# Split-precision decoder trunk: token halves of the last output column in PSUM tiles of their own, another division of the norms' work between VectorE and ScalarE, and an earlier start of the FFN's second k-group

## The chip, the cores and the metric

The kernel runs on one core of one Trainium2 chip. The metric is the device time of one execution in microseconds (us); shown are the median of three runs and, beside it, one profiled execution. Engines are named as in the profile: PE (TensorE's matmuls), DVE (VectorE), ACT (ScalarE), POOL (GpSimd) and SP (SyncE, which issues the DMAs).

## The reference

Two layers of a decoder trunk on 256 tokens of width 2048 in float32, every sub-layer behind an RMS norm that a conditioning vector shifts, scales and gates:

```
def rms_norm(x, g, eps=1e-6):
    return x * lax.rsqrt(jnp.mean(x * x, axis=-1, keepdims=True) + eps) * g

for layer in range(DEPTH):                                   # DEPTH = 2
    mod = (silu(c) @ ada_w[layer] + ada_b[layer])[:, None, :]
    sh_m, sc_m, g_m, sh_f, sc_f, g_f = jnp.split(mod, 6, axis=-1)
    hm = rms_norm(x, norm_mix_g[layer]) * (1.0 + sc_m) + sh_m
    y = ab_mixer(hm, ...) if layer == 0 else cd_mixer(hm, ...)    # w_in -> heads -> w_out
    x = x + (1.0 + g_m) * y
    hf = rms_norm(x, norm_ffn_g[layer]) * (1.0 + sc_f) + sh_f
    x = x + (1.0 + g_f) * swiglu(hf, w_gate, w_up, w_down)        # D_FF = 5632
```

## The kernel before

**Linears.** Every float32 product is made of three matmuls on rounded halves: `hi*h + hi*l + lo*h`. A weight slab (two k-tiles of 128 rows, 512 columns, 512 KB) is loaded into a `raw` tile by SP's queue, copied to `hi` by ACT (L311) and subtracted to `lo` by DVE (L316); of `raw` there are four buffers, of `hi` and `lo` three each. In `dense_as` the tokens stand still in PE and the weights stream: a PSUM tile `accps` of two banks holds the two token halves of 128, and a slab costs 12 matmuls of 512 columns (2 k-tiles, 3 products, 2 halves). A linear goes over its output in column blocks of 512. In the last block (`b == 3`) of a linear that adds to the residual stream, called the tail here, the last two slabs are done together, 12 matmuls for token half 0 first and then 12 for half 1.

**Residual and norm.** `residual` multiplies the PSUM tile by a gate (L848), adds to `xr` (L852) and has ACT take the squares for the next norm (`Stats`, L876, with Sqrt at L885 and DVE's reciprocal at L890). `Norm` then makes the next linear's stationary tiles, per k-tile: `scale` multiplies tokens by the reciprocal root (the first 512 columns on DVE, L916, the others on ACT, L914), PE transposes 128x128 pieces into a `pm` tile (PSUM, one bank, L149), ACT's `high` makes `h` (L920) and DVE's `low` makes a value `t` (L926) and `l = t - h` (L927). Both of these read the same PSUM tile:

```
h = A.activation(self.hs[k][0][:, dst], ps, AF.Identity, bias=..., scale=self.gs[k])
V.tensor_scalar(t, ps, self.gs[k], modcol(self.layer, self.sh, k), op0=OP.mult, op1=OP.add)
V.tensor_tensor(l[:, dst], t, h[:, dst].bitcast(F32), op=OP.subtract)
```

`head(cc)` does this for the first four k-tiles of token half `cc`, inside the first two slabs of the next linear; `pair(j)` does it for k-tiles 2j and 2j+1 of both halves, one pair per slab from then on. This happens in three places, which the text calls by their reciprocal roots: f0 (`rstdf`, after the output projection of layer 0, before FFN 0), m1 (`rstdm`, after FFN 0, before layer 1's mixer) and f1 (`rstdf`, after layer 1's output projection, before FFN 1).

**FFN 0 in two k-groups.** FFN 0 reads its weights for the first eight k-tiles over twelve column blocks (group 1), then for the other eight (group 2), adding to the sums kept in SBUF. `grouped(..., early=1)` queues the `pair`s of group 2 at the start of the last block of group 1.

**Order.** Python order within priorities gives each engine's program. `tc.issue_after(x)` keeps an instruction behind `x` on its engine. `pace` and `npace` are a list and a count by which a slab's split is kept behind the norm work of the pair before it, so that the splits don't run ahead of the pairs. `W_AHEAD` is the priority lead of a slab's load and split.

## Time and profile before

| what | value |
|---|---|
| median of three runs | 2621.95 us (2621.33 to 2623.5) |
| the profiled execution's own time | 2620.44 us |
| its span, first to last instruction | 2618.7 us |
| mean granted clock of PE, as a share of full speed | 0.992 |
| PE, DVE, ACT busy | 2564.7, 1887.3, 1244.0 us |
| DMA | 672.97 MB, 257 GB/s on the mean |

The span is from the first to the last instruction on the core; the execution's own time is 1.7 us more. The waits of an engine are idle time by what ended it. A window's row gives an engine's busy time with its count of instructions and the granted clock. In a timeline row, instructions of one line that follow each other are joined (x4), and the bracket gives the idle time before the first and what ended it.

### The profile page before, as it was taken

How to read it: one execution, taken by the hardware profiler on the slowest of the kernel's cores; microseconds unless marked ns; L12 is line 12 of the kernel's file. 1: busy time of each engine (PE TensorE's matmuls, PEld its weight loads, DVE VectorE, ACT ScalarE, POOL GpSimd, SP SyncE). 2: the span in 40 equal slices, each digit the busy share in tenths (PEclk: the TensorE clock that was granted, in tenths of full speed). 3: DMA queues.
4: the chain of work that ended last, by engine and by line, in shares of the span. 5: the costliest groups of instructions: out<-in, count | busy, mean ns of one | idle time of the engine just before them, and what ended most of it. 6: DMA issues, size and time to landing. Idle time of an engine off the chain costs nothing.

```text
span 2618.7 us, 35776 instructions
## 1 busy us (share of the span) xinstructions
PE 2564.7 (98%) x13669; PEld 2198.0 (84%) x13669; DVE 1887.3 (72%) x2046; ACT 1244.0 (48%) x1566; POOL 5.2 (0%) x19
## 2 busy tenths in 40 slices
PE   6999999999999999999999999999999999999999
PEld 5999899988787888888888799998688888888887
DVE  6899887889777887777777687767674455544554
ACT  4534866645544444344444545544544443344443
POOL 0000000000000000000000000000000000000000
PEclk8999999999999999999999999999999999999999
DMA  8998677889697989999898588788676666666665
GB/s 313 336 337 292 187 216 225 271 276 329 224 329 271 325 299 312 319 316 310 299 303 313 176 270 279 249 266 277 196 256 193 187 191 199 201 190 191 190 202 162
DMA packets 307798, 672.97 MB, mean 257 GB/s; under 512 B 24016, under 2 KB 26538, under 8 KB 307626
## 3 DMA queue, kind: packets, MB, share of 16 engines
q1 hardware_dynamic: 307338, 670.60, 78.1%
q8 instruction: 107, 1.75, 0.3%
q14 instruction: 65, 0.53, 0.1%
q10 hardware_dynamic: 288, 0.08, 0.0%
HBM read 668.46 MB, written 2.13 MB: 256 GB/s over the span
## 4 chain that ended last, share of the span: by engine, by line
PE 94%; DVE 2%; ACT 2%; DMA 2%; issue 1%; SPq 0%; DVEq 0%; ACTq 0%
PE accps L158 71%; PE accps L358 18%; PE pm L158 4%; PE pm L149 1%; DMA blk<-in_ada_w 1%; ACT h L920 1%; DVE lo L316 1%; ACT hi L311 1%; DVE t L926 0%; DMA raw<-in_ab_w_in 0%; DMA xr<-in_x 0%; DMA hb<-in_ssd_a_log 0%; DVE blk L316 0%; DVE l L927 0%; PE pm L687 0%
## 5 line engine op out<-in xcount | busy, mean ns | idle before, releaser
L311 ACT ACTIVATE hi<-raw 128x1024 fp32r<-128x1024 f32 (+1 forms) x875 | 913.8, 1046 | 1188.6 <-PE accps L158 922.1
L316 DVE TENSOR_TENSOR lo<-raw,hi 128x1024 fp32r<-128x1024 f32 (+1 forms) x875 | 1052.8, 1206 | 565.2 <-ACT hi L311 556.8
L158 PE MATMUL accps<-hi,h 128*128 128x512 f32 x1908 | 524.2, 394 | 13.6 <-ACT hi L311 6.4
L158 PE MATMUL accps<-hi,l 128*128 128x512 f32 x1908 | 518.1, 392 | 0.0
L158 PE MATMUL accps<-lo,h 128*128 128x512 f32 x1908 | 515.0, 391 | 0.0
L206 DVE SCALAR_TENSOR_TENSOR acc<-araw,ct,acc 128x1024 f32<-128x1024 f32 (+2 forms) x377 | 465.5, 1235 | 14.5 <-DMA araw<-in_ada_w 13.6
L158 PEld LDWEIGHTS accps<-hi,h 128*128 128x128 f32 x1908 | 354.1, 188 | 93.6 <-ACT h L920 15.1
L158 PEld LDWEIGHTS accps<-hi,l 128*128 128x128 f32 x1908 | 357.6, 188 | 76.6 <-DVE l L927 2.8
L158 PEld LDWEIGHTS accps<-lo,h 128*128 128x128 f32 x1908 | 358.5, 189 | 75.0 <-issue 0.2
L158 PE MATMUL accps<-hi,blk 128*128 128x512 f32 x1664 | 413.6, 390 | 0.0
L358 PE MATMUL accps<-h,lo 128*128 128x256 f32 x1408 | 380.3, 285 | 3.1 <-DVE lo L316 3.1
L358 PE MATMUL accps<-h,hi 128*128 128x256 f32 x1408 | 380.0, 285 | 2.2 <-ACT h L473 1.7
L358 PE MATMUL accps<-l,hi 128*128 128x256 f32 x1408 | 378.7, 285 | 0.0
L158 PEld LDWEIGHTS accps<-hi,blk 128*128 128x128 f32 x1664 | 311.7, 188 | 64.4
L358 PEld LDWEIGHTS accps<-h,hi 128*128 128x128 f32 x1408 | 262.4, 192 | 4.8 <-ACT h L473 1.8
L358 PEld LDWEIGHTS accps<-h,lo 128*128 128x128 f32 x1408 | 261.8, 192 | 4.7 <-DVE lo L316 3.8
L358 PEld LDWEIGHTS accps<-l,hi 128*128 128x128 f32 x1408 | 261.8, 192 | 1.1 <-issue 0.2
L158 PE MATMUL accps<-lo,blk 128*128 128x512 f32 x832 | 223.5, 389 | 0.0
L158 PEld LDWEIGHTS accps<-lo,blk 128*128 128x128 f32 x832 | 156.1, 188 | 32.4
L512 DVE TENSOR_TENSOR blk<-accps,blk 128x1024 f32<-128x1024 f32 x40 | 48.7, 1218 | 5.4 <-PE accps L158 5.2
L848 DVE TENSOR_TENSOR blk<-accps,gate 128x1024 f32<-128x1024 f32 (+1 forms) x27 | 29.7, 1104 | 29.6 <-PE accps L158 28.1
L926 DVE TENSOR_SCALAR t<-pm,gs,mod 128x256 f32<-128x256 f32 (+1 forms) x60 | 29.3, 488 | 25.5 <-ACT h L920 25.5
(247 smaller groups left out, 1098.1 us busy)
## 6 DMA issues: line engine op xcount, KB each, us to landing
araw<-in_ada_w SPq DMA_DIRECT2D x323, 512.0 KB, 5.5
raw<-in_ffn_w_gate SPq DMA_DIRECT2D x176, 512.0 KB, 4.4
raw<-in_ffn_w_up SPq DMA_DIRECT2D x176, 512.0 KB, 4.5
raw<-in_ffn_w_down SPq DMA_DIRECT2D x176, 512.0 KB, 4.8
raw<-in_ab_w_in SPq DMA_DIRECT2D x130, 512.0 KB, 5.1
raw<-in_cd_w_in SPq DMA_DIRECT2D x96, 512.0 KB, 4.8
raw<-in_ab_w_out SPq DMA_DIRECT2D x64, 512.0 KB, 5.6
raw<-in_cd_w_out SPq DMA_DIRECT2D x32, 512.0 KB, 5.7
```

Source lines behind the costliest of these rows:

```text
L149: T.transpose(dst, src, ident)
L158: return T.matmul(o, a, b, start=first, stop=last, skip_group_check=True)
L206: V.scalar_tensor_tensor(acc, r, ct[nr][:, g:g + 1], acc, op0=OP.mult, op1=OP.add)
L311: A.activation(hi, raw, AF.Copy)
L316: wlast[1] = V.tensor_tensor(lo, raw, hi.bitcast(F32), op=OP.subtract)
L358: dense_mm[0] = T.matmul(acc[:, n, :], a[:, n * P:(n + 1) * P], b, start=first and n % 2 == 0, stop=final, skip_group_check=True)
L512: V.tensor_tensor(dst, acc, dst, op=OP.add)
L848: V.tensor_tensor(y[:, c, :], acc[:, c, :], g[:, None, :].to_broadcast([P, c.stop - c.start, 512]), op=OP.mult)
L920: return A.activation(self.hs[k][0][:, dst], ps, AF.Identity, bias=modcol(self.layer, self.sh, k), scale=self.gs[k]).ins
L926: V.tensor_scalar(t, ps, self.gs[k], modcol(self.layer, self.sh, k), op0=OP.mult, op1=OP.add)
```

## The change

1. In the tail each token half has a `pm` tile of its own in place of one `accps` tile, and half 0's multiply and add no longer share a tile with half 1. At the end of the kernel, half 0 is added and stored, then half 1.
2. `prefetch` loads and splits three slabs of the next linear before the tail's first add (in `before`, two slabs, one of them split by DVE behind that add, and the third later). The second and the third have buffers of their own (`own`) and are not paced.
3. `head` has two `pm` tiles with two transposes each; the first 512 columns of token half 1 are scaled by ACT.
4. In `pair`, DVE alone reads the transposes: two values, then ACT copies them to `h`, then two `low`s. The scale of the next 512 columns goes with each pair, so a pair's transposes are there one slab earlier.
5. `grouped` has `early=2`: the pairs of group 2 are queued two blocks (eight slabs) ahead, without pace.

```diff
-            after = pace[2 * npace[0] - 1] if 0 < 2 * npace[0] <= len(pace) else None
+            after = pace[2 * npace[0] - 1] if 0 < 2 * npace[0] <= len(pace) and not own else None
...
+    def prefetch(w, c0):
+        for j in range(3):
+            ready.append(wslab(w, 2 * j, 2, c0, 512, W_AHEAD, own=j > 0))
+        return wlast[1].ins
...
-        acc = psA.tile([P, 1024], F32, tag="acc", name="accps").rearrange("p (n t) -> p n t", n=2)
+        if tail:
+            accs = [pm(), pm()]
...
-                made.append((run, *wslab(w, run[0][0], len(run), c0, 512, ahead, own=begin and j == 1)))
+                made.append((run, *(ready.popleft() if ready else wslab(w, run[0][0], len(run), c0, 512, ahead))))
...
-                if begin and j == 0:
-                    head(n)
+                if begin and (n, j) in ((0, 0), (0, len(ops) - 2)):
+                    head(int(j > 0))
...
+        if isinstance(acc, list):
+            with (tc.issue_after(after) if after else ExitStack()):
+                add(0)
+            if store:
+                nc.sync.dma_start(out[0, 0:P, c0:c0 + 512], xr[:, 0, c0:c0 + 512])
+                add(1)
+                nc.sync.dma_start(out[0, P:S, c0:c0 + 512], xr[:, 1, c0:c0 + 512])
+            else:
+                stats.add(0, b)
+                stats.end(0)
+                stats.second = lambda: add(1)
+            return
...
+        def value(self, k, ps, t):
+            return V.tensor_scalar(t, ps, self.gs[k], modcol(self.layer, self.sh, k), op0=OP.mult, op1=OP.add).ins
...
-                ps = pm()
+                two = [pm(), pm()]
...
+                ts = [t1(), t1()]
                 for i in range(2):
-                    k = 2 * j + i
-                    pace.append((self.high(k, ps[:, i * S:(i + 1) * S], slice(0, S)),
-                                 self.low(k, ps[:, i * S:(i + 1) * S], slice(0, S))))
-                self.last = pace[-1]
+                    self.value(2 * j + i, ps[:, i * S:(i + 1) * S], ts[i])
+                for i in range(2):
+                    act = A.activation(self.hs[2 * j + i][0], ts[i], AF.Copy).ins
+                for i in range(2):
+                    dve = self.low(2 * j + i, ts[i], slice(0, S))
+                self.scale(c + 1, j % 2)
...
+        after = prefetch(ffn_w_gate[0], 0) if b == 3 else None
...
-    hf = grouped(fblocks, FGROUPS, 0, 3, makef, finishf, F_RATES, (LAGS[-1], LAGS[-1]), normf.head, 1)
+    hf = grouped(fblocks, FGROUPS, 0, 3, makef, finishf, F_RATES, (LAGS[-1], LAGS[-1]), normf.head, 2)
```

DVE's program around m1's first add, before: `lo` rows are splits of slabs (of the tail, at first), `blk<-raw,blk` the split of a prefetched slab with its own buffers, L848 and L852 the multiply and the add of a token half.

```order
L316 TENSOR_TENSOR lo<-raw,hi 128x1024 [waits DMAHW4_49,PE_49,Activation_49]
L316 TENSOR_TENSOR lo<-raw,hi 128x1024 [waits DMAHW6_49,PE_49,Activation_49]
L848 TENSOR_TENSOR blk<-accps,gate 128x512 [waits PE_49]
L852 TENSOR_TENSOR xr<-blk,xr 128x512 [waits DVE_49]
L316 TENSOR_TENSOR blk<-raw,blk 128x1024 [waits DMAHW7_49,Activation_49]
L890 RECIPROCAL rstdm_12342<-rstdm_12342 128x1 [waits Activation_49]
L916 TENSOR_SCALAR t_13268<-xr,rstdm_12342 128x256 [waits DVE_49]
```

The same place after the change, where L869 and L872 are the multiply and the add and L951 the scale; the four splits are those of the first slab with its own buffers, of the tail's last slab, of the second slab with its own buffers, and of the prefetched slab in the common buffers:

```order
L316 TENSOR_TENSOR blk<-raw,blk 128x1024 [waits DMAHW7_49,Activation_49]
L316 TENSOR_TENSOR lo<-raw,hi 128x1024 [waits DMAHW4_49,PE_49,Activation_49]
L316 TENSOR_TENSOR blk<-raw,blk 128x1024 [waits DMAHW0_49,Activation_49]
L316 TENSOR_TENSOR lo<-raw,hi 128x1024 [waits DMAHW6_49,PE_49,Activation_49]
L869 TENSOR_TENSOR blk<-pm,gate 128x512 [waits PE_49]
L872 TENSOR_TENSOR xr<-blk,xr 128x512 [waits DVE_49]
L924 RECIPROCAL rstdm_12345<-rstdm_12345 128x1 [waits Activation_49]
L951 TENSOR_SCALAR t_13280<-xr,rstdm_12345 128x256 [waits DVE_49]
```

So three splits of prefetched slabs stand ahead of the first add, where one stood and another followed it; the text calls the two with their own buffers p1 and p2 and the one in the common buffers p0, and the tail's last slab sn.

PE's program in m1 at a pair's place, before: L149 are the transposes into a `pm` tile, L158 the matmuls of a slab.

```order
L158 MATMUL accps<-lo,h_13225 128x512 x2
L149 MATMUL pm<-ident,t_13394 128x128 [waits Activation_49]
L149 MATMUL pm<-ident,t_13394 128x128
L149 MATMUL pm<-ident,t_13396 128x128 [waits Activation_49]
L149 MATMUL pm<-ident,t_13394 128x128
L149 MATMUL pm<-ident,t_13396 128x128 x2
L149 MATMUL pm<-ident,t_13394 128x128
L149 MATMUL pm<-ident,t_13396 128x128
L158 MATMUL accps<-hi,h_13227 128x512 [waits Activation_49]
```

And after:

```order
L158 MATMUL accps<-lo,h_13247 128x512 x2
L149 MATMUL pm<-ident,t_13369 128x128
L149 MATMUL pm<-ident,t_13390 128x128
L149 MATMUL pm<-ident,t_13369 128x128
L149 MATMUL pm<-ident,t_13390 128x128
L158 MATMUL accps<-hi,h_13249 128x512 [waits Activation_49]
```

Before, the eight transposes of two pairs stand right ahead of the matmuls that need the first of them. After, four transposes stand between two slabs' matmuls, and they belong to the pair of the slab after the next.

PE's program in FFN 0 where the first matmul of group 2 comes, before (`h_8407` is the first tile of group 2, and `t_8494` and `t_8496` are sources of its transposes):

```order
L149 MATMUL pm<-ident,t_8494 128x128 [waits Activation_49]
L149 MATMUL pm<-ident,t_8496 128x128 [waits Activation_49]
L149 MATMUL pm<-ident,t_8494 128x128
L149 MATMUL pm<-ident,t_8496 128x128
L158 MATMUL accps<-lo,h_7401 128x512 [waits DVE_49]
...
L158 MATMUL accps<-hi,h_7405 128x512 [waits Activation_49]
...
L158 MATMUL accps<-lo,h_7407 128x512 x2
L158 MATMUL accps<-hi,h_8407 128x512 [waits PE_49,Activation_49]
```

And after, where `h_8325` is that tile:

```order
L158 MATMUL accps<-hi,h_7412 128x512 [waits Activation_49]
L158 MATMUL accps<-hi,h_7412 128x512
L158 MATMUL accps<-hi,h_7414 128x512 x2
L158 MATMUL accps<-hi,l_7413 128x512 x2
L158 MATMUL accps<-hi,l_7415 128x512 x2
L158 MATMUL accps<-hi,h_8325 128x512 [waits Activation_49]
```

The transposes of group 2 have left the last block of group 1; they stand in the block ahead of it, four after each of its slabs.

## Rows read from the trace of the kernel before

**Rows 1.** The page: the span, and busy time of each engine.

```profile
span 2618.7 us, 35776 instructions
PE 2564.7 (98%) x13669; PEld 2198.0 (84%) x13669; DVE 1887.3 (72%) x2046; ACT 1244.0 (48%) x1566; POOL 5.2 (0%) x19
```

**Rows 2.** PE's waits: line, releaser, us in total, times, longest us.

```profile
PE pm L149 <- DVE t L916: 9.6, 3, 3.2
...
PE accps L158 <- ACT hi L311: 6.4, 5, 2.5
PE accps L158 <- ACT h L920: 6.4, 14, 0.6
```

**Rows 3.** Windows: length; PE, PEld, DVE, ACT, POOL busy (instructions); PEclk, DMA share, GB/s.

```profile
696.87:716.00 19.13, 14.52 (x60) 10.37 (x60) 16.41 (x38) 11.42 (x24) 0.00 (x0) 0.91 0.23 64
...
828.04:851.69 23.65, 18.25 (x77) 13.95 (x76) 17.87 (x25) 14.20 (x19) 0.00 (x0) 0.93 0.50 158
...
1452.42:1491.43 39.01, 32.77 (x134) 23.14 (x135) 30.53 (x59) 23.56 (x41) 0.00 (x0) 0.91 0.34 102
...
1866.02:1901.70 35.68, 29.42 (x119) 20.46 (x119) 27.51 (x56) 20.90 (x39) 0.00 (x0) 0.90 0.32 89
```

**Rows 4.** The chain that ended last, and PE's timeline at eight transposes.

```profile
1170.23 43.55 PE accps L158 x192
...
1474.23 1.04 PE L149 MATMUL pm<-ident,t 128*128 128x128 f32 x8
```

**Rows 5.** Timeline of m1's head: start and length in us.

```profile
1451.80 0.61 PE L158 MATMUL accps<-lo,blk 128*128 128x512 f32 x2
1452.45 0.69 DVE L848 TENSOR_TENSOR blk<-accps,gate 128x512 f32<-128x512 f32 x1 [4.03 <-PE accps L158]
...
1455.18 0.62 DVE L916 TENSOR_SCALAR t<-xr,rstdm 128x256 f32<-128x256 f32 x2
...
1455.59 1.12 PE L149 MATMUL pm<-ident,t 128*128 128x128 f32 x4 [3.18 <-DVE t L916]
...
1457.26 1.22 PE L158 MATMUL accps<-hi,h 128*128 128x512 f32 x2 [0.55 <-ACT h L920]
...
1468.07 1.16 PE L158 MATMUL accps<-hi,h 128*128 128x512 f32 x4
```

**Rows 6.** Timeline of DVE in m1's tail.

```profile
1441.76 1.23 DVE L316 TENSOR_TENSOR lo<-raw,hi 128x1024 fp32r<-128x1024 f32 x1 [1.50 <-ACT hi L311]
```

**Rows 7.** Slab transfers issued at 1438.2 and at 1448.2: last number is us to landing.

```profile
raw<-in_cd_w_in SPq DMA_DIRECT2D x1, 512.0 KB, 6.7
...
raw<-in_cd_w_in SPq DMA_DIRECT2D x1, 512.0 KB, 4.3
```

**Rows 8.** Groups by form: busy us, mean ns | idle before, and what ended it.

```profile
L311 ACT ACTIVATE hi<-raw 128x1024 fp32r<-128x1024 f32 x847 | 896.7, 1060 | 1169.9 <-PE accps L158 919.6 <-PE accps L358 173.3 <-DMA raw<-in_ab_w_in 27.1
...
L920 ACT ACTIVATE h<-pm,mod,gs 128x256 fp32r<-128x256 f32 x36 | 20.2, 562 | 27.3 <-DVE t L926 17.1 <-PE pm L149 10.1
...
L926 DVE TENSOR_SCALAR t<-pm,gs,mod 128x256 f32<-128x256 f32 x36 | 19.5, 542 | 17.5 <-ACT h L920 17.5
...
L927 DVE TENSOR_TENSOR l<-t,h 128x256 fp32r<-128x256 f32 x36 | 15.3, 425 | 1.2
...
L926 DVE TENSOR_SCALAR t<-pm,gs,mod 128x128 f32<-128x128 f32 x24 | 9.7, 406 | 7.9 <-ACT h L920 7.9
...
L914 ACT ACTIVATE t<-xr,rstdf 128x512 f32<-128x512 f32 x12 | 8.2, 717 | 0.5 <-DVE rstdf L890 0.5
...
L927 DVE TENSOR_TENSOR l<-t,h 128x128 fp32r<-128x128 f32 x24 | 7.0, 292 | 0.7
...
L420 ACT ACTIVATE h<-blk 128x256 fp32r<-128x256 f32 x16 | 6.2, 410 | 0.3 <-PE accps L358 0.2
```

**Rows 9.** Timeline of the kernel's end.

```profile
2612.53 1.29 DVE L848 TENSOR_TENSOR blk<-accps,gate 128x512 f32<-128x512 f32 x2 [6.75 <-PE accps L158]
2613.73 1.28 DVE L852 TENSOR_TENSOR xr<-blk,xr 128x512 f32<-128x512 f32 x2
```

More of the change, by code (lines that the diff above doesn't have):

```diff
@@ L402, in dense_as @@
                     pump()
-        return acc
+        return accs if tail else full
     def flip(src, use):
@@ L838, in gate_tile, with residual, add @@
         return g
-    def residual(acc, g, b, scale=None, stats=None, store=False):
+    def residual(acc, g, b, scale=None, stats=None, store=False, after=None):
         y = tb()
-        cols = slice(512 * b, 512 * (b + 1))
-        tail = b == 3 and (stats is not None or store)
-        def add(c):
+        c0 = 512 * b
+        def add(cc):
+            xc = xr[:, cc, c0:c0 + 512]
             if scale is None:
-                V.tensor_tensor(y[:, c, :], acc[:, c, :], g[:, None, :].to_broadcast([P, c.stop - c.start, 512]), op=OP.mult)
+                V.tensor_tensor(y[:, cc, :], acc[cc], g, op=OP.mult)
@@ L849, in add @@
             else:
-                for cc in range(c.start, c.stop):
-                    V.scalar_tensor_tensor(y[:, cc, :], acc[:, cc, :], scale[:, cc:cc + 1], g, op0=OP.mult, op1=OP.mult)
-            return V.tensor_tensor(xr[:, c, cols], y[:, c, :], xr[:, c, cols], op=OP.add).ins
-        for c in ([slice(0, 1), slice(1, 2)] if tail and store else [slice(0, 1 if tail else 2)]):
-            add(c)
-            for cc in range(c.start, c.stop):
-                if store:
-                    nc.sync.dma_start(out[0, cc * P:(cc + 1) * P, cols], xr[:, cc, cols])
-                if stats is not None:
-                    stats.add(cc, b)
@@ L861, in residual @@
[L861 to L863 removed]
+                V.scalar_tensor_tensor(y[:, cc, :], acc[cc], scale[:, cc:cc + 1], g, op0=OP.mult, op1=OP.mult)
+            return V.tensor_tensor(xc, y[:, cc, :], xc, op=OP.add).ins
+        if isinstance(acc, list):
[5 more added lines that the diff above has]
+                nc.sync.dma_start(out[0, P:S, c0:c0 + 512], xr[:, 1, c0:c0 + 512])
+            else:
+                stats.add(0, b)
+                stats.end(0)
+                stats.second = lambda: add(1)
+            return
@@ new lines, in residual @@
+        if scale is None:
+            V.tensor_tensor(y, acc, g[:, None, :].to_broadcast([P, 2, 512]), op=OP.mult)
+        else:
+            for cc in range(2):
+                V.scalar_tensor_tensor(y[:, cc, :], acc[:, cc, :], scale[:, cc:cc + 1], g, op0=OP.mult, op1=OP.mult)
+        xc = xr[:, :, c0:c0 + 512]
+        V.tensor_tensor(xc, y, xc, op=OP.add)
+        for cc in range(2):
+            if store:
+                nc.sync.dma_start(out[0, cc * P:(cc + 1) * P, c0:c0 + 512], xr[:, cc, c0:c0 + 512])
+            if stats is not None:
+                stats.add(cc, b)
@@ L932, in head @@
             with tc.high_priority(offset=600):
-                with (tc.issue_after(self.last[1]) if cc else ExitStack()):
-                    dve = self.scale(0, cc)
                 if cc == 0:
@@ L1045, in ffn_out @@
             acc = dense_as(ffn_w_down[layer], 512 * b, a, tail=tail)
+            after = prefetch(*then) if then and tail else None
             with tc.high_priority(offset=600):
-                residual(acc, g, b, None, stats, store)
+                residual(acc, g, b, None, stats, store, after)
     normf = Norm(stats, 0, 3, cols[1], 32)
@@ L1053, in makef @@
             hs = normf.slots(k0, kg)
-        normf.queue(k0 // 2 if k0 else 2, kg // 2 if k0 else kg // 2 - 2)
+        if k0:
+            preps.append(lambda: [normf.scale(k0 // 4, cc) for cc in range(2)])
+        normf.queue(k0 // 2 if k0 else 2, kg // 2 if k0 else kg // 2 - 2, not k0)
         return hs
```

102 lines of the change are left out of this document (62 added, 40 removed).

## Prediction

> **What bounds the kernel now.** I read the busy times first: PE is busy for 98% of the span, DVE for 72%, ACT for 48% [rows 1]. Nearly all of the time is PE's matmuls, and the change removes none of them, so it can only win where PE stands still or runs slowly. The list of PE's waits names such places: 9.6 us in three waits for the norm's first scaled tile, 6.4 us in five waits for ACT's `hi` [rows 2]. These three norms are f0 (before FFN 0), m1 (before layer 1's mixer) and f1 (before FFN 1); the other place is FFN 0's step from its first eight k-tiles to the second eight ("group 2"). Named waits are not the whole loss, since PE also runs there at a lower granted clock, 0.90 to 0.93 on the mean [rows 3]. So I set each stretch against its content at full speed. A full-speed matmul takes 43.55/192 = 0.2268 us and a transpose 1.04/8 = 0.13 us [rows 4]. The counts in [rows 3] hold 16 transposes in f0 and in group 2, and 32 in m1 and in f1; four of m1's matmuls are the 256-column kind, put at half, 0.12 us:
>
> - f0: 19.13 - 44 x 0.2268 - 16 x 0.13 = 7.1 us lost
> - group 2: 23.65 - 61 x 0.2268 - 16 x 0.13 = 7.7 us
> - m1: 39.01 - 98 x 0.2268 - 4 x 0.12 - 32 x 0.13 = 12.1 us
> - f1: 35.68 - 87 x 0.2268 - 32 x 0.13 = 11.8 us
>
> Together 38.7 us, and some 6.2 us more at the very end, from PE's last matmul, which releases DVE at 2612.5, to the end of the span [rows 1, 9]. This is all that there is to win.
>
> **A: from the last matmul of the tail to the first of the next linear.** In m1 the tail's last matmul ends at 1451.80 + 0.61 = 1452.42 (I call it E) and the first head matmul starts at 1457.26, 4.84 us later. Between them stand the add of token half 0 (from 1452.45), Square, Sqrt and the scale, the transposes from 1455.59, and ACT's `h` [rows 5]. The add reads only half 0, whose matmuls end 12 x 0.2268 = 2.72 us before E, yet it waited for half 1, which lies in the same PSUM tile. With a tile each, it can start at E - 2.72 at the earliest. But the order on DVE puts the splits of the prefetched slabs p1, p2 and p0 ahead of it. p2's transfer needs the buffer that the split at 1441.76 frees, at 1442.99 [rows 6]; two transfers of this size in the neighbourhood landed after 4.3 and 6.7 us [rows 7]. At 4.5 us, ACT's split (1.06) [rows 8] and DVE's of p2 and p0 (2 x 1.23) end at 1451.0, so the add starts at about E - 1.4. I take the value near the lower landing, because the tail leaves the queue less to move; the bounds are E - 2.7 and, at 6.7 us, E + 0.8. From add to transposes stays 3.14 us. Then ACT starts after two transposes of four, saving half of their 1.12 us: 1.67 - 0.56 = 1.11. The first matmul then comes at -1.4 + 3.14 + 1.11 = 2.85 us after E, a gain of 2.0. I take the same for f1. In f0 p0's split stands ahead of p2's, so that less is queued before the add: 2.5. **Gain 6.5** (bounds: nothing with the add at E + 0.8, where 2.0 - 2.2 is about zero; 10.4 with it at E - 2.7, which is 1.3 more in each).
>
> **B: the rest of the head.** From m1's first head matmul to the first after the first pair 10.81 us pass [rows 5], for 24 matmuls, 4 transposes of the second half and 8 of the pairs: 24 x 0.2268 + 12 x 0.13 = 7.0. The 3.8 us over that are a chain on DVE: the second add, 0.62 for the second half's scale, eight times value and low (0.41 + 0.29 [rows 8]) and a slab's split of 1.23. The change moves the scale to ACT and the split ahead of the add: 0.62 + 1.23 = 1.85 off the chain. Two tiles for the four transposes also let the readers work apart: DVE's 128-wide values waited 7.9 us for ACT's `h` in the three norms [rows 8], 2.6 each, of which I count a third, 0.85. That makes 2.7 for m1; I take the same for f1. In f0 ACT also scales the second group's column slabs there (its 512-wide scale takes 0.72 [rows 8], and five come ahead of the copies that the second part waits for), which gives back most: 1.0. **Gain 6.4** (bounds 3 and 9).
>
> **C: pairs.** What is left in m1 is 12.1 - 4.8 - 3.8 = 3.5 us, and as much in f1. The order on PE shows why: a pair's transposes stood right ahead of its own matmuls, and PE waited for `h`; now they stand one slab ahead. Per slab PE then needs 12 x 0.2268 + 4 x 0.13 = 3.24 us. DVE needs two values, two lows and a split, 2 x 0.54 + 2 x 0.43 + 1.23 = 3.17, and ACT two copies, a split and a scale, 2 x 0.41 + 1.06 + 0.72 = 2.6 [rows 8]. So both fit beside PE, DVE with hardly any room. The copy of `t` to `h` is hidden by the 3.24 us of look-ahead; without that cover it is a rival below. **Gain 7.0** (bounds 0 and 7.0).
>
> **D: group 2.** The loss was 7.7 us, mostly waits for slabs' `hi` (up to 2.5 us each, [rows 2]), whose splits stood in ACT's and DVE's order behind the group's own norm work. Now that work is done in the last two blocks of group 1, its transposes in the first of these, and nothing is paced against it, so the slabs' splits are not held. DVE has about 2 us too much to do over these four slabs, hidden by the slabs split ahead. I leave 0.3 for the step. **Gain 7.4** (bounds 3 and 7.7).
>
> **E: the end.** The first half's multiply and add (0.65 + 0.64 [rows 9]) are done while the second half's matmuls still run, and so the last store is issued about one us earlier. **Gain 1.0** (bounds 0 and 1.3).
>
> The sum is 6.5 + 6.4 + 7.0 + 7.4 + 1.0 = 28.3 us. The profiled execution took 2620.44 us, so 2592.1; the median of the runs shown is 1.5 above it, which makes **2594 us**.
>
> **Rivals.**
>
> *The clock.* In m1 0.91 over 39.01 us is some 7.0 us at half speed, in f1 7.1, in f0 3.4 [rows 3]. It fell after PE had stood for 3.2 us [rows 5]. In the changed kernel the longest stand is 1.7 us before the transposes and about 0.6 behind them, and I forecast that the clock mostly holds afterwards. If it falls as before, PE loses up to half of that time times its share of work, of which most is under DVE's chain anyway: 1.6 to 2 us in each norm, 2599.
>
> *The first add stays late.* If p2 lands after 6.7 us or more, the add starts at E + 0.8, behind where it stands now, and A loses 2.2 us in each norm, B perhaps 1 of the same chain: 8 to 9 us, 2603. For it speaks that one transfer nearby took that long; against it that the other took 4.3.
>
> *DVE's value, then ACT's copy, as a chain.* Before, ACT's `h` from PSUM took 0.56 us; now value and copy follow each other, 0.54 + 0.41 = 0.95 [rows 8]. If a pair's result is needed at once because DVE has fallen behind, each of 14 pairs costs 0.39 more: 5.5 us, 2599. On the same 128x256 tile in PSUM, DVE's value took 542 ns and ACT's `h` 562, so by the rows DVE loses nothing as the reader. The Trainium skill (ScalarE: Activation LUTs, "Step-by-step: what each stage is for") says "ScalarE is closer to PSUM, VectorE is closer to SBUF", which speaks against giving DVE all PSUM reads and ACT the SBUF ones; by that rule the chain would be longer than these rows make it and this rival likelier, but the trace disagrees by those 20 ns.
>
> *No change.* If DVE's queue, not the shared tiles, holds the norms (p2 late, the pairs bound by DVE's 3.17 us per slab plus whatever else it is given), A to C win nothing; and if group 2's stall only moves into the last two blocks of group 1, whose slabs' splits would then wait behind the norm's work on DVE, D wins nothing either: 2622.
>
> *Slower.* On ACT p1's split now stands ahead of that of the tail's last slab, sn. The tail needs sn at E - 24 x 0.2268 + 6 x 0.2268 = E - 4.08 = 1448.34, so p1 must have landed by 1448.34 - 2 x 1.06 = 1446.2. It is issued one slab before p2, at 1442.99 - 2.72 = 1440.3: 5.9 us. Each us beyond that holds PE in the tail. To cost more than the whole gain, it would have to land 28.3/3 = 9.5 us too late in all three norms, after some 15 us; the longest in [rows 7] is 6.7. Then 2627 or more.
>
> **How the numbers follow.** The forecast 0.52, with a range of its own of 2589 to 2599; the clock 0.18; the late add 0.10; the chain through DVE 0.10; no change 0.05; slower 0.05. The late add with one of the others reaches 2608, and A and B at their upper bounds (3.9 and 2.6 more) give 2587: that is the range, 2587 to 2608. Some 0.2% (5 us) is what a measurement of this kernel can tell from no change; faster by more than that 0.90, within it 0.05, slower 0.05.
>
> **What the changed profile would show.** A: PE's idle time before the head's transposes falls from 3.2 to about 1.7 us, with DVE's add starting before the tail's last matmul ends. B: some 8 us instead of 10.8 between the first head matmul and the first after a pair. C: PE's 14 waits for `h` [rows 2] gone, DVE without idle time in the pairs. D: no wait for `hi` in FFN 0's second group. Clock: above 0.95 in the norm stretches. E: the span ends about 5 us after the last matmul. I would be wrong if PE waits in the tail for `hi`, if DVE's splits come late in the pairs, or if a wait in group 1's last two blocks takes the place of group 2's.

## The result and the profile after

The changed kernel takes 2595.8 us (median; 2593.3 to 2596.5) against 2622.7 of the kernel before measured beside it, a ratio of 0.9896 (95% interval 0.9879 to 0.9913). Forecast were 2594 and 2587 to 2608. Its profiled execution took 2596.0 us, 24.4 less than that of before.

The page of the changed kernel, its span and busy times:

```profile
span 2594.3 us, 35777 instructions
PE 2554.7 (98%) x13669; PEld 2196.6 (85%) x13669; DVE 1882.3 (73%) x2040; ACT 1242.4 (48%) x1572; POOL 5.2 (0%) x19
```

The work is the same (13669 matmuls); only PE's standing and slow time shrank. PE's waits in the changed kernel (line, releaser, us in total, times, longest), to be held against [rows 2]:

```profile
PE pm L149 <- DVE t L951: 6.1, 3, 2.5
...
PE accps L158 <- ACT hi L311: 1.7, 2, 0.9
...
PE accps L158 <- ACT h L957: 0.8, 3, 0.3
```

The wait for the first scaled tile fell from 9.6 to 6.1 us, not to about 5 as 3 x 1.7 would have it; the 14 waits for `h` of [rows 2] are 3, and none of the two that are left for slabs' `hi` stands in group 2. The four windows of [rows 3], each from the end of the same matmul to the end of the same matmul (f0, group 2, m1, f1):

```profile
699.45:716.80 17.35, 14.36 (x59) 10.69 (x60) 13.21 (x34) 13.92 (x29) 0.00 (x0) 0.90 0.21 69
...
827.54:844.25 16.71, 16.71 (x78) 13.83 (x77) 16.71 (x24) 9.81 (x14) 0.00 (x0) 1.00 0.87 285
...
1445.84:1475.90 30.06, 27.74 (x134) 21.82 (x135) 25.90 (x55) 22.31 (x43) 0.00 (x0) 1.00 0.42 131
...
1850.47:1878.87 28.40, 26.35 (x120) 20.69 (x120) 23.09 (x52) 20.17 (x41) 0.00 (x0) 0.94 0.37 110
```

Group 2 has nothing left to win: PE is busy for all of its 16.71 us at the full clock. The granted clock is full in m1 too, but 0.90 in f0 and 0.94 in f1.

Since both kernels run 13669 matmuls, the k-th matmul of one trace can be set beside the k-th of the other, which gives the difference by stretch. The columns are: from the start to f0's E; from f0's E (end of the tail's last matmul) to the matmul at 740 us of before; group 2, from there to that at 1000 us; m1's tail, from that at 1440 us to E; m1, from E to that at 1500 us; f1, from E to that at 1910 us; and from the last matmul to the end of the span. "After less before", us; the other rows belong to the experiments below, and all have the kernel before as their base:

| kernel | start | f0 | group 2 | m1 tail | m1 | f1 | end |
|---|---|---|---|---|---|---|---|
| after | +2.6 | -1.8 | -8.2 | +0.8 | -9.0 | -7.6 | -1.3 |
| u_group2 | -0.5 | -2.3 | +7.6 | +0.6 | -7.8 | -7.4 | -1.3 |
| u_early1 | +1.8 | -4.0 | -8.2 | +0.6 | -8.1 | -7.4 | -1.3 |
| u_paced2 | -0.1 | -2.4 | +6.0 | +0.8 | -9.0 | -7.4 | -1.3 |
| o_group2 | +0.3 | +0.8 | -8.2 | 0.0 | +0.1 | +0.1 | 0.0 |
| u_tile | +2.7 | -1.3 | -8.2 | +0.8 | -6.3 | -6.5 | 0.0 |
| u_readers | -0.4 | -1.4 | -8.2 | +0.4 | -8.4 | -6.8 | -1.3 |
| u_look | +2.8 | -2.3 | -8.2 | 0.0 | -5.9 | -6.7 | -1.3 |
| u_prefetch | +1.6 | -4.2 | -8.2 | 0.0 | -9.5 | -9.3 | -1.3 |
| x_slot | +3.6 | -5.1 | -8.2 | 0.0 | -10.3 | -7.7 | -1.3 |
| x_p1 | +2.1 | -2.2 | -8.2 | 0.0 | -8.2 | -7.4 | -1.3 |
| x_fill | -0.7 | -3.7 | -8.2 | +0.4 | -9.1 | -8.1 | -1.3 |
| x_mix | +1.3 | -4.8 | -8.2 | +1.0 | -10.2 | -9.3 | -1.3 |

The column "start" moves by up to 4.3 us between kernels whose code does not differ there, so single spans and medians can't be compared below that; what the change does is read from the other columns. They sum to 27.1 us for the changed kernel, where 28.3 were forecast.

Each row is one execution, and the other columns have a spread of their own. u_group2, u_early1 and u_paced2 differ from the changed kernel in group 2 alone, so in the three norms they repeat it: f0 goes from -1.8 to -4.0, m1 from -7.8 to -9.0, f1 from -7.4 to -7.6. A difference inside these spreads can't be put down to an edit. Two things make them, and both can be read apart. The first is the time at which p1 lands: in f0 of these four executions the first add starts 0.65 to 1.57 us before E, and the first matmul of the head moves with it. The second is the clock in the head, which here is the stretch from the first matmul behind E, transposes not counted, to the 25th (the first after the first pair). With the clock full the head takes 8.2 us in m1, in the changed kernel and in u_paced2; with the clock fallen it takes 9.3 and 9.1, in u_group2 and u_early1. The experiments below are therefore read in three pieces: from E to the first head matmul, the head, and the rest.

m1 in the changed kernel (timeline; start, length), beside [rows 5]:

```profile
1438.86 1.06 ACT L311 ACTIVATE blk<-raw 128x1024 fp32r<-128x1024 f32 x1 [4.54 <-DMA raw<-in_cd_w_in]
...
1439.96 1.23 DVE L316 TENSOR_TENSOR blk<-raw,blk 128x1024 fp32r<-128x1024 f32 x1 [4.38 <-ACT blk L311]
...
1440.78 1.04 ACT L311 ACTIVATE blk<-raw 128x1024 fp32r<-128x1024 f32 x1
...
1441.10 1.22 DVE L316 TENSOR_TENSOR lo<-raw,hi 128x1024 fp32r<-128x1024 f32 x1
...
1442.23 1.22 DVE L316 TENSOR_TENSOR blk<-raw,blk 128x1024 fp32r<-128x1024 f32 x1
...
1442.37 0.73 PE L158 MATMUL pm<-lo,blk 128*128 128x512 f32 x2 [0.24 <-DVE lo L316]
...
1443.37 1.22 DVE L316 TENSOR_TENSOR lo<-raw,hi 128x1024 fp32r<-128x1024 f32 x1
...
1444.51 0.68 DVE L869 TENSOR_TENSOR blk<-pm,gate 128x512 f32<-128x512 f32 x1
...
1447.73 0.63 PE L149 MATMUL pm<-ident,t 128*128 128x128 f32 x4 [1.89 <-DVE t L951]
...
1448.69 0.85 PE L158 MATMUL accps<-hi,h 128*128 128x512 f32 x2 [0.33 <-ACT h L957]
...
1456.87 1.19 PE L158 MATMUL accps<-blk,h 128*128 128x512 f32 x4
```

The add starts at 1444.51, 1.3 us before E = 1445.84, and the first head matmul comes 2.85 us behind E, as forecast. The head lasts 1456.87 - 1448.69 = 8.2 us, forecast some 8. The cost stands ahead of that: ACT stood for p1's transfer until 1438.86, DVE then did the splits of p1, sn, p2 and p0 in a row (1439.96, 1441.10, 1442.23, 1443.37), PE waited for sn's `lo` until 1442.37, and the tail became 0.8 us longer. In f0 the same queue came out worse:

```profile
694.29 1.06 ACT L311 ACTIVATE blk<-raw 128x1024 fp32r<-128x1024 f32 x1 [2.81 <-DMA raw<-in_ffn_w_gate]
...
695.38 1.23 DVE L316 TENSOR_TENSOR blk<-raw,blk 128x1024 fp32r<-128x1024 f32 x1 [2.64 <-ACT blk L311]
696.52 1.22 DVE L316 TENSOR_TENSOR lo<-raw,hi 128x1024 fp32r<-128x1024 f32 x1
697.66 1.22 DVE L316 TENSOR_TENSOR blk<-raw,blk 128x1024 fp32r<-128x1024 f32 x1
698.79 0.74 DVE L871 SCALAR_TENSOR_TENSOR blk<-pm,rby,gate 128x512 f32<-128x512 f32 x1
...
701.99 0.77 PE L149 MATMUL pm<-ident,t 128*128 128x128 f32 x4 [2.54 <-DVE t L951]
702.97 1.15 PE L158 MATMUL accps<-hi,h 128*128 128x512 f32 x2 [0.22 <-ACT h L957]
```

p1 was there only at 694.29, three splits followed each other on DVE, and the add came at 698.79, 0.65 us before E = 699.45: later against E than in m1, where the forecast had it earlier.

### The profile page after: what moved, and what is told of

Read it like the earlier page. It is cut to its first block, busy times and chain, and to the rows that moved or that the text cites. A ratio compares the mean times of both kernels' runs of the same rounds, so it can differ in the third digit from the quotient of the medians.

```text
span 2594.3 us, 35777 instructions
## 1 busy us (share of the span) xinstructions
PE 2554.7 (98%) x13669; PEld 2196.6 (85%) x13669; DVE 1882.3 (73%) x2040; ACT 1242.4 (48%) x1572; POOL 5.2 (0%) x19
## 4 chain that ended last, share of the span: by engine, by line
PE 95%; DMA 2%; DVE 1%; ACT 1%; issue 0%; SPq 0%; DVEq 0%
PE accps L158 69%; PE accps L358 19%; PE pm L158 6%; PE pm L149 1%; DMA blk<-in_ada_w 1%; DMA raw<-in_ffn_w_gate 0%; DVE lo L316 0%; DMA raw<-in_ab_w_in 0%; DMA xr<-in_x 0%; DMA raw<-in_cd_w_in 0%; DMA t<-in_gm_ln_g 0%; DMA hb<-in_ssd_a_log 0%; ACT hi L311 0%; ACT h L957 0%; PE pm L708 0%
## 5 line engine op out<-in xcount | busy, mean ns | idle before, releaser
L158 PE MATMUL accps<-hi,h 128*128 128x512 f32 x1864 | 507.0, 393 | 2.8 <-ACT hi L311 1.7
L158 PE MATMUL accps<-hi,l 128*128 128x512 f32 x1864 | 503.7, 390 | 0.0
L158 PE MATMUL accps<-lo,h 128*128 128x512 f32 x1864 | 501.9, 390 | 0.0
L158 PEld LDWEIGHTS accps<-hi,l 128*128 128x128 f32 x1864 | 349.6, 188 | 72.7
L158 PEld LDWEIGHTS accps<-lo,h 128*128 128x128 f32 x1864 | 349.4, 188 | 72.7 <-issue 0.2
L158 PEld LDWEIGHTS accps<-hi,h 128*128 128x128 f32 x1864 | 346.4, 188 | 75.0 <-ACT h L957 3.8
L158 PE MATMUL accps<-hi,blk 128*128 128x512 f32 x1440 | 357.3, 390 | 0.0
L158 PEld LDWEIGHTS accps<-hi,blk 128*128 128x128 f32 x1440 | 269.6, 188 | 55.8
L158 PE MATMUL accps<-lo,blk 128*128 128x512 f32 x720 | 192.6, 389 | 0.0
L158 PEld LDWEIGHTS accps<-lo,blk 128*128 128x128 f32 x720 | 135.1, 188 | 28.0
L158 PE MATMUL pm<-hi,blk 128*128 128x512 f32 x224 | 56.4, 390 | 0.0
L158 PEld LDWEIGHTS pm<-hi,blk 128*128 128x128 f32 x224 | 42.0, 188 | 9.1 <-ACT hi L311 0.4
```

The source lines that it names most:

```text
L158: return T.matmul(o, a, b, start=first, stop=last, skip_group_check=True)
```

## The experiments

Each is an edit of the changed kernel, but for o_group2, which edits the kernel before. Ratios are to the kernel before, run beside it.

**u_group2: place and pace of group 2 undone.**

```diff
-    hf = grouped(..., normf.head, 2)
+    hf = grouped(..., normf.head, 1)
-            if not (early and gi):
-                new_pace(QUIET if sh else 0)
+            new_pace(QUIET if sh and gi == 0 else 0)
-        normf.queue(..., not k0)
+        normf.queue(...)
```

> The changed kernel with its fifth part undone: FFN 0's second group is queued one block ahead and paced, as before; the pairs keep their new readers. Theory (the place decides): the group's norm work again stands among the slabs' splits of the last block and holds them, so most of the 6.9 us that this stretch won in the profile comes back: the stretch from the end of the last-but-one block to the first block of group 2 is 5 to 7 us longer, the median about 2601 to 2603. Rival (the readers decide): before, ACT and DVE took turns on one PSUM tile, and that made the norm work too long for one block; with DVE alone as the reader one block is enough, and the stretch is at most 2 us longer, the median within 2 us of the changed kernel's 2595.8.

2608.8 us, 0.9948 (0.9935 to 0.996). Neither theory: 15.8 us worse than the changed kernel in this stretch and 7.6 worse than before. Its timeline shows why:

```profile
829.13 0.87 ACT L1022 ACTIVATE h<-t 128x256 fp32r<-128x256 f32 x2 [2.72 <-DVE t L960]
...
829.90 1.04 ACT L311 ACTIVATE hi<-raw 128x1024 fp32r<-128x1024 f32 x1
...
831.00 1.19 PE L158 MATMUL accps<-hi,h 128*128 128x512 f32 x4 [2.48 <-ACT hi L311]
```

A slab's `hi` stands right behind the pair's copies on ACT, and PE waits 2.48 us for it, four times. That this is longer than before with the same pace fits the new pairs, whose copies come behind both of DVE's values; it was not tried by itself. So place and pace had to be told apart.

**u_early1: the place alone undone; u_paced2: the pace alone undone; o_group2: this part alone on the kernel before.**

```diff
 # u_early1
-    hf = grouped(..., normf.head, 2)
+    hf = grouped(..., normf.head, 1)
 # u_paced2
-            if not (early and gi):
-                new_pace(QUIET if sh else 0)
+            new_pace(QUIET if sh and gi == 0 else 0)
-        normf.queue(..., not k0)
+        normf.queue(...)
 # o_group2, on the kernel before: early 1 -> 2, no new_pace for group 2,
 # and in pair(j, paced):
-            with ..., tc.issue_after(self.last[0]), tc.issue_after(self.last[1]):
+            with ..., (tc.issue_after(self.last[0]) if paced else ExitStack()), ...:
```

> The changed kernel with FFN 0's second group queued one block ahead, as before, but unpaced: only the place is undone. The run with place and pace undone lost some 15 us against the changed kernel in this stretch, and there PE waited four times about 2.5 us for a slab's hi that stood behind the copies of a pair. Theory (the pace made those waits): without it the splits run ahead and the stretch is at most 2 us longer than in the changed kernel; median 2594 to 2598. Rival (the place did: five pieces of norm work don't fit beside four slabs, and DVE is late): 4 to 8 us longer, median 2600 to 2604.

2596.8 us, 0.9907 (0.9892 to 0.9922): the stretch is as short as in the changed kernel, -8.2. The place does nothing.

> The changed kernel with FFN 0's second group queued two blocks ahead, but paced, as before: only the pace is undone. Theory (the pace holds a slab's split behind the copies of the pair that goes with it): the waits of about 2.5 us for hi are there again, now in the last block but one, and the stretch is 8 to 15 us longer; median 2604 to 2611. Rival (with two blocks there is time enough, and the pace holds nothing): within 2 us of 2595.8.

2607.7 us, 0.9946 (0.9933 to 0.9958): +6.0 in the stretch, 14.1 worse than unpaced. Its list of PE's waits has, where the changed kernel has 1.7 us:

```profile
PE accps L158 <- ACT hi L311: 10.8, 5, 2.5
```

> The kernel before with the fifth part of the change alone: FFN 0's second group is queued two blocks ahead and unpaced, with ACT and DVE both reading the transposes as before. Theory (the place decides): the stretch around group 2 wins 5 to 7 us as in the changed kernel, median 2615 to 2617. Rival (it needs the new readers too): the norm work, now spread over two blocks, still holds the slabs' splits, and at most 3 us are won: 2619 or more.

2613.6 us, 0.997 (0.9959 to 0.9981): -8.2 with the old readers too. In group 2 the pace was the whole loss.

**u_tile: one PSUM tile for both halves again.**

```diff
         if tail:
-            accs = [pm(), pm()]
+            full = psA.tile([P, 1024], F32, tag="acc", name="accps").rearrange("p (n t) -> p n t", n=2)
+            accs = [full[:, 0, :], full[:, 1, :]]
```

> The changed kernel with the two token halves of the tail in one PSUM tile of two banks again; the order of instructions otherwise kept. Theory (the shared tile holds the first add): DVE's first multiply waits for the tail's last matmul, so the head starts later by the lead that the first add has in the changed kernel: 1.3 us in m1, 1.5 in f1, 0.65 in f0, and the end by 1.3; with that, longer idle time before the transposes brings the half clock back in m1 too. Median 2600 to 2603. Rival (the splits set the start, and the tile nothing): the head starts as in the changed kernel, and the median is within 1.5 us of 2595.8.

2600.9 us, 0.9915 (0.9902 to 0.9929). The theory held. The first head matmul comes later behind E by 1.3 us in m1, 1.6 in f1 and 0.7 in f0, and the end by 1.3: 4.9 us for the shared tile. By stretch the loss is 2.6 in m1, 1.1 in f1 and 0.5 in f0, with the end 5.5, because in m1 the clock fell too (head 9.5 us for 8.2) and in f1 and f0 the heads were 0.5 and 0.2 us shorter. PE's wait in m1 is back at the 3.18 us of [rows 5]:

```profile
1449.55 0.70 PE L149 MATMUL pm<-ident,t 128*128 128x128 f32 x4 [3.18 <-DVE t L952]
```

**u_readers: ACT reads PSUM for `h` again. u_look: the scale back in its own pair.**

```diff
 # u_readers
-                    act = A.activation(self.hs[2 * j + i][0], ts[i], AF.Copy).ins
+                    act = self.high(2 * j + i, ps[:, i * S:(i + 1) * S], slice(0, S))
 # u_look
+                for cc in range(2):
+                    self.scale(c, cc)
                 ps = pm()
...
-                self.scale(c + 1, j % 2)
```

> The changed kernel with ACT making h from the PSUM tile in a pair, as before, while DVE still makes both values from it first; the transposes keep their look-ahead of a slab. Theory (the look-ahead made the pairs' gain): m1 and f1 stay within 1 us of the changed kernel, since the added turn-taking is hidden under the slab of matmuls between a pair's transposes and its own matmuls; median within 2 us of 2595.8. Rival (the readers made it): ACT's h waits for both values and DVE's next values for ACT, the waits of PE for h come back, and m1 and f1 lose 3 us or more each: median 2602 or more.

2594.3 us, 0.9895 (0.9882 to 0.9909): f0, m1 and f1 lose 0.4, 0.6 and 0.8 us, m1's tail wins 0.4. f1's 0.8 lie ahead of the first head matmul, where the edit changes nothing; m1's 0.6 lie in the head, at the full clock in both. With the look-ahead in place, who reads the transposes in the pairs is worth 0.6 us in a norm at most.

> The changed kernel with the scale of 512 columns back at the start of the pair that needs it, ahead of its own transposes; DVE alone still reads the transposes. PE's order then has two pairs' transposes together right ahead of the matmuls, as before. Theory (the look-ahead made the gain of the pairs): PE waits again for h at every second pair, and m1 and f1 lose 2.5 to 3.5 us each, the median about 2601 to 2603. With the chain of value, copy now longer than ACT's own read of PSUM it may even be more. Rival (the readers or the splits made it): less than 1 us each, median under 2598.

2599.0 us, 0.9911 (0.9898 to 0.9925): m1 lost 3.0, f1 0.9, while m1's tail won 0.8 and f0 0.5, both with the changed kernel's own order there. Both losses are mixed with the clock, which fell in m1's head and stayed full in f1's, the other way round than in the changed kernel. The rest behind the head is free of that: it takes 21.0 us for 19.0 in m1 and 18.3 for 16.3 in f1, so 2.0 us lost in each. m1's rest in the kernel before, the changed kernel and u_look (windows):

```profile
1468.07:1491.43 23.36, 21.49 (x97) 15.09 (x96) 18.46 (x30) 15.52 (x23) 0.00 (x0) 1.00 0.38 113
...
1456.87:1475.90 19.03, 19.03 (x95) 15.76 (x95) 17.70 (x30) 14.09 (x23) 0.00 (x0) 1.00 0.48 142
...
1456.79:1477.80 21.01, 19.49 (x95) 15.78 (x95) 17.60 (x30) 14.58 (x23) 0.00 (x0) 1.00 0.43 128
```

The waits for a copied `h` are back:

```profile
PE accps L158 <- ACT h L1025: 3.0, 4, 0.8
```

So the look-ahead is about half of the pairs' gain of 4.3 us in m1 and 3.9 in f1. What made the other half was not tried by itself: the readers were undone only with the look-ahead in place.

**u_prefetch: no prefetch of three slabs.**

```diff
-        for j in range(3):
-            ready.append(wslab(w, 2 * j, 2, c0, 512, W_AHEAD, own=j > 0))
-        return wlast[1].ins
+        return None
...
-                made.append((run, *(ready.popleft() if ready else wslab(w, run[0][0], len(run), c0, 512, ahead))))
+                made.append((run, *(ready.popleft() if ready else wslab(w, run[0][0], len(run), c0, 512, ahead, own=begin and j == 1))))
```

> The changed kernel without the prefetch of three slabs: the next linear's first two slabs are split when the scheduler puts them (the second in buffers of its own, as before), the third in the head. Theory (the split of the third slab and of the second lay on DVE's chain in the head): the first add comes up to 1.3 us earlier than now, at the end of half 0, but the head is longer by one or two splits of 1.22 us, and the matmuls of the third slab wait for them: 1 to 2.5 us lost in each norm, median 2599 to 2603. Rival (the early add is worth more than the split, whose place is free behind the add): the norms are as long or shorter, median 2593 to 2597.

2589.5 us, 0.9876 (0.9863 to 0.989): the rival, and more than it said. By stretch the prefetch costs 2.4 us in f0, 0.8 in m1's tail, 0.5 in m1 and 1.7 in f1, 5.4 together. In pieces: without it the first head matmul comes 2.0, 1.3 and 1.2 us sooner behind E in f0, m1 and f1. At the full clock the head is longer without it, as the theory had it, but by less than one split: 9.0 us for 8.2 in m1, and 9.0 in f1 for the 8.1 of x_fill below. In f0 and f1 the clock of the changed kernel had also fallen, which cost some 1.3 us each (x_fill), so 2.6 of the 5.4 us are the clock's; against u_early1, whose clock stayed full in f0, the prefetch costs 0.2 us there. f1's timeline without the prefetch:

```profile
1843.19 0.69 DVE L867 TENSOR_TENSOR blk<-pm,gate 128x512 f32<-128x512 f32 x1 [1.31 <-PE pm L158]
...
1844.53 1.22 DVE L316 TENSOR_TENSOR blk<-raw,blk 128x1024 fp32r<-128x1024 f32 x1
...
1846.34 0.70 PE L149 MATMUL pm<-ident,t 128*128 128x128 f32 x4 [0.47 <-DVE t L949]
...
1847.33 0.84 PE L158 MATMUL accps<-hi,h 128*128 128x512 f32 x2 [0.29 <-ACT h L955]
```

The add starts the moment half 0 is done (it waits for PE), the split stands behind it in the time in which ACT makes Square and Sqrt, and PE stands for 0.47 us, not 1.67.

**x_slot: the third split behind the first add. x_p1: in m1, ACT's splits of prefetched slabs behind that of the tail's last slab.**

```diff
 # x_slot
-        for j in range(3):
+        for j in range(2):
             ready.append(wslab(w, 2 * j, 2, c0, 512, W_AHEAD, own=j > 0))
-        return wlast[1].ins
+        return wlast[1].ins, lambda behind: ready.append(wslab(w, 4, 2, c0, 512, W_AHEAD, own=True, behind=behind))
...
-                add(0)
+                first = add(0)
+            if after:
+                after[1](first)
 # x_p1
+        tail_hi = ahi[0]
         for j in range(3):
-            ready.append(wslab(w, 2 * j, 2, c0, 512, W_AHEAD, own=j > 0))
+            ready.append(wslab(w, 2 * j, 2, c0, 512, W_AHEAD, own=j > 0, behind=tail_hi))
```

> The changed kernel, with the split of the third prefetched slab on DVE moved from ahead of the tail's first add to behind it, where DVE waits for ACT's Square and Sqrt anyway. Theory (the first add is held by the third split, not by half 0): the add starts about 1.1 us earlier in each of the three norms (E - 2.6 in m1 and f1, E - 1.8 in f0), PE's idle time before the transposes falls from 2.5, 1.9 and 1.7 us to about 1.4, 0.8 and 0.6, and the median falls by 3 us, to about 2592.5, by 2 more if the half clock in f0 and f1 goes too. Rival: the split behind the add delays the reciprocal and the scale by as much as the add won, or the transfers land so late that the add waits for the second split anyway: 2595 to 2597.

2590.0 us, 0.9881 (0.9868 to 0.9895). f0 won 3.3 us (2.0 ahead of the first head matmul and 1.2 in the head, whose clock stayed full), m1 with its tail 2.1 (1.3 ahead of the first head matmul, 0.8 in the tail), f1 only 0.1: there p1's transfer was late again and the clock fell as before.

> The changed kernel, with ACT's splits of the prefetched slabs held behind ACT's split of the tail's last slab. It changes the order on ACT in m1 alone. Theory (in m1 the tail's last slab waited on ACT behind the first prefetched slab, which had not landed, and PE stood for it): m1's tail loses its stall of about 1.0 us, the rest is the same; median about 1 us under 2595.8. Rival: the last slab itself came late, or DVE's split of it does, and the tail stays as long: no change.

2594.5 us, 0.9896 (0.9882 to 0.9909): no change. The stall in m1's tail went away (0.8; it did so in u_look too, with the old order), and the first head matmul came 0.3 us sooner behind E, but m1 lost as much again: its first matmuls ran at the half clock there, which they did not in the changed kernel, and the head took 9.3 us. The edit did not bring that about by itself: u_group2 and u_early1, which have the changed kernel's own m1, took 9.3 and 9.1.

```profile
1445.75 0.63 PE L149 MATMUL pm<-ident,t 128*128 128x128 f32 x4 [1.58 <-DVE t L954]
...
1446.71 1.22 PE L158 MATMUL accps<-hi,h 128*128 128x512 f32 x2 [0.33 <-ACT h L960]
```

**x_fill: matmuls that nobody reads, in PE's idle time.**

```diff
                 if cc == 0:
+                    fill = psA.tile([P, 1024], F32, tag="acc", name="fillps")
+                    with tc.issue_after(dense_mm[0].ins):
+                        for _ in range(7):
+                            mm(fill[:, 0:512], fills[0][:, 0:P], fills[1][:, 0, :])
```

> The changed kernel with seven more matmuls of 512 columns (1.6 us) into a PSUM tile that nobody reads, right behind the tail's last matmul, in the time in which PE stands idle before the head's transposes. The output is not touched. Theory (the idle time lowers the clock, and the low clock costs): the half clock of 3.4 us in f0 and in f1 goes away, and the two heads are shorter by 1 to 1.7 us each, median 2592.5 to 2594. Rival 1 (the head is bound by DVE and ACT, not by PE): the clock stays full and the heads stay as long, no change. Rival 2: the clock falls all the same, since the busy time before or after decides; no change, or 1 us more for the added matmuls' own wait.

2593.8 us, 0.9893 (0.988 to 0.9907), not to be told from the changed kernel by its median. By stretch (the added matmuls left out of the count) f0 won 1.9 us and f1 0.5; m1, whose clock had been full, 0.1 and its tail 0.4. f0's and f1's windows:

```profile
696.15:711.58 15.43, 14.71 (x66) 10.44 (x65) 12.56 (x33) 13.92 (x29) 0.00 (x0) 1.00 0.18 63
...
1844.84:1872.74 27.90, 26.68 (x126) 20.42 (x126) 23.83 (x54) 20.22 (x41) 0.00 (x0) 1.00 0.40 118
```

The clock is 1.00 where it was 0.90 and 0.94. The stretches mix this with p1's landing: against the changed kernel's profile the first head matmul came 0.6 us sooner behind E in f0 and 0.8 later in f1. The heads alone show what the clock cost: 8.34 us for 9.59 in f0, 8.14 for 9.47 in f1, and in m1, where the clock had been full, 8.19 for 8.18. f1's head in the changed kernel and here:

```profile
1853.13:1862.60 9.47, 9.37 (x36) 6.86 (x36) 6.59 (x21) 5.96 (x16) 0.00 (x0) 0.82 0.02 6
...
1848.32:1856.46 8.14, 8.12 (x36) 5.63 (x36) 6.60 (x21) 5.97 (x16) 0.00 (x0) 1.00 0.01 4
```

DVE and ACT are as busy in the one as in the other. So the theory held, with 1.3 us in each of the two heads, and rival 1 did not. That the added matmuls kept the clock up is not shown by f0 alone, where it stayed full in u_early1 without them; in f1 it fell in every run that had the prefetch in f1 and no such matmuls, but for u_look.

**x_mix: x_slot in f0 and m1, no prefetch in f1.**

```diff
+ (the edit of x_slot)
-        after = prefetch(ffn_w_gate[1], 0) if b == 3 else None
+        after = None
```

> A version made of what the runs favour: in f0 and m1 the third prefetched slab is split behind the first add, in f1 there is no prefetch; all else as in the changed kernel. From the profiles, counted from the tail of layer 0's output projection on, f0 wins 3.2 us against the changed kernel, m1 2.1 and f1 1.7: 7 us, median about 2589. Rival (f1's gain without prefetch came from the clock, which falls or not by chance): 5 us, and no better than the two single versions, 2590 to 2592.

2588.4 us, 0.9873 (0.9859 to 0.9886): the fastest, 7.4 us under the changed kernel by the medians, though its interval does not part it from u_prefetch and x_slot. By stretch it wins 3.0 us in f0, 1.2 in m1 and 1.7 in f1 and keeps the stall in m1's tail, 5.7 together and so between the two expectations; f1's gain came as in u_prefetch, 1.2 us of it ahead of the first head matmul. The clock is full in all three norms; f0's, m1's and f1's windows:

```profile
698.18:712.48 14.30, 13.15 (x59) 9.47 (x59) 12.54 (x33) 13.08 (x27) 0.00 (x0) 1.00 0.24 68
...
1441.72:1470.58 28.86, 27.68 (x134) 21.81 (x135) 25.87 (x55) 21.34 (x41) 0.00 (x0) 1.00 0.44 140
...
1845.18:1871.94 26.76, 25.15 (x120) 19.45 (x120) 23.98 (x53) 20.11 (x39) 0.00 (x0) 1.00 0.44 124
```

## Why the prediction was right, and where not

The time came out because the places of the loss were right and because the errors of the five terms cancelled, which is luck: A brought 5.2 us for 6.5, B 4.1 for 6.4, C 9.2 for 7.0, D 8.2 for 7.4 and E 1.3 for 1.0, and 0.8 were lost in m1's tail, which the sum had at nothing.

- **A, from tail to head** (6.5): the first head matmul came 2.85 us behind E in m1, as worked out, 2.65 in f1 and 3.5 in f0, where 4.5 were before, so 1.0 for 2.5. In f1 the step was the one forecast: ACT waited for p2's transfer last, if only for 0.23 us, and p2's and p0's splits on DVE followed (the two rows below are ACT's splits of p1 and p2). In m1 the number is right by another path. p2 was there in time (ACT split it at 1440.78 without a wait), and p1 was late, so that four splits of DVE stood in a row in front of the add; E moved out with them, since PE waited for sn's split among the four, and the add's lead of 1.3 us on E is what PE still had to do from sn's `lo` on (3.5 us) less the two splits behind sn's on DVE (2.1 us). That this equals the forecast is luck. In f0 the step that failed is "less is queued before the add": p1's landing came so late that three splits of DVE stood in a row in front of it. How late it comes differs between executions: in the other runs with the same order in f0, the first head matmul came 2.6 to 3.5 us behind E, never at the 2.0 that were forecast. The step also took the splits ahead of the add as a price that had to be paid. u_prefetch and x_slot show that it need not be: a split behind the first add lies under ACT's Square and Sqrt.

```profile
1844.34 1.06 ACT L311 ACTIVATE blk<-raw 128x1024 fp32r<-128x1024 f32 x1 [1.84 <-DMA raw<-in_ffn_w_gate]
1845.63 1.06 ACT L311 ACTIVATE blk<-raw 128x1024 fp32r<-128x1024 f32 x1 [0.23 <-DMA raw<-in_ffn_w_gate]
```

- **B, the rest of the head** (6.4): m1 8.2 us for "some 8" and 10.8 before, a gain of 2.6; f1 9.5 for 10.55, 1.1; f0 9.6 for 10.0, 0.4. What B had wrong is that all the time above the matmuls' own was a chain on DVE. The clock was a part of it: before, m1's head ran at 0.76 of full speed on the mean, and of its 2.6 us about 1 is there only because the clock now stayed full, as the 9.3 and 9.1 us of the same head in u_group2 and u_early1 show. f1 is longer than m1 by its clock alone: in x_fill, at the full clock, f1's head takes 8.14 us. The term that moved the splits "off the chain" was booked as a gain, yet the prefetch as a whole cost 5.4 us: it saved some 0.9 in a head at the same clock, and took more than that from the first add and the tail, and the clock took its part. m1's head before and after (windows):

```profile
1457.26:1468.07 10.81, 10.16 (x37) 7.32 (x37) 7.50 (x22) 5.78 (x14) 0.00 (x0) 0.76 0.32 100
...
1448.69:1456.87 8.18, 8.08 (x36) 5.64 (x37) 6.54 (x21) 5.97 (x16) 0.00 (x0) 1.00 0.09 34
```

- **C, pairs** (7.0): behind the head, m1 took 19.0 us for 23.4 and f1 16.3 for 20.2, 8.3 us, and 0.9 more were won in f0 and behind f1's window. That is above the bound of 7.0, which was set too low: the 4.8 us that it takes off hold four transposes, 0.5 us of work in each norm, and the counts of [rows 3] take in matmuls that only touch a window's edge. Counted from end to end, f0, group 2, m1 and f1 hold 41, 60, 96 and 86 full-size matmuls where the prediction has 44, 61, 98 and 87, so that their losses come to some 40 us, not 38.7. u_look bears out the look-ahead for 2.0 us in each of m1 and f1; the rest of the gain is not shown to be the look-ahead's. In the list of groups DVE still has idle time ahead of the pairs' values, 1.8 us in all, and they took what was forecast, so 3.17 us per slab was no bound yet:

```profile
L961 DVE TENSOR_SCALAR t<-pm,gs,mod 128x256 f32<-128x256 f32 x36 | 17.9, 539 | 1.8 <-PE pm L149 1.8
```

- **D, group 2** (7.4): 8.2, all that there was (7.9 by the counts just given). Place and pace were named together; the pace alone did it.
- **E, the end** (1.0): 1.3.
- **The rivals.** The clock: forecast above 0.95 in the norm stretches, it fell to 0.90 in f0 and 0.94 in f1 and not in m1; by the heads of x_fill this cost 1.3 us each, in all half of the 5 us put on it. The slower case (p1's split ahead of sn's, with PE waiting in the tail, one of the signs of being wrong) took place in m1's tail at 0.8 us, with the mechanism as told; its 15 us of landing were far off. The Trainium skill's sentence (ScalarE: Activation LUTs, "Step-by-step: what each stage is for") that ScalarE is the one closer to PSUM would, as the prediction read it, have made the new readers a loss; u_readers, with ACT as a reader again, did not win in any norm.

The sum of the stretches, 27.1, fits the medians (2622.7 - 2595.8 = 26.9); the profiled execution showed 24.4 because its start took 2.6 us longer, in code that the change leaves alone.

## What to carry to other kernels

A slab split ahead of time is not free where its split stands, in an engine's fixed order, in front of the instruction that ends a chain: find the slot in which that engine waits anyway, and put it there. Undo the parts of a change one at a time, and set the k-th matmul of one trace beside the k-th of the other: that shows where a difference lies, though medians of the whole kernel drown it. Then see how much the same stretch differs between runs that leave it alone (up to 2.2 us here), and cut it into pieces whose spread has a cause that can be read, here a transfer's landing and the granted clock, before a difference is put down to an edit. An order constraint that was written to protect a stretch (the pace) can be the whole of its loss.

## What the runs showed of the hardware

A stand of PE did not by itself decide whether the clock fell. m1's head is the same program in the changed kernel and in u_group2, and in both PE stood for 1.89 us, made four transposes in 0.63 us and waited 0.33 us for `h`. In the changed kernel the clock stayed at 2.4 GHz (1.00 in the head, whose first two matmuls took 0.85 us). In u_group2 the same two took 1.22 us and the head's mean was 0.82, part of it at 1.2 GHz:

```profile
1459.58 0.63 PE L149 MATMUL pm<-ident,t 128*128 128x128 f32 x4 [1.89 <-DVE t L950]
1460.53 1.22 PE L158 MATMUL accps<-hi,h 128*128 128x512 f32 x2 [0.33 <-ACT h L956]
...
1460.53:1469.86 9.33, 9.23 (x36) 6.82 (x36) 6.52 (x21) 5.96 (x16) 0.00 (x0) 0.82 0.12 38
```

Behind a shorter stand, 1.58 us in m1 of x_p1, it fell too. The Trainium skill (TensorE: Matmul & The Clock Gate, "Part 1: The HAM clock gate") says that activity is judged in a free-running rhythm that no kernel start resets; by that the same code may or may not meet a fall. These rows agree with it, and no run here shows the rhythm itself. With stands of at most 0.8 us (all three norms of u_prefetch and x_mix, f0 and m1 of x_slot), and with x_fill's matmuls in the gap, the clock fell in none of these. Where it fell, a head of the changed kernel's own program took 0.8 to 1.5 us longer than at the full clock.
